# Output projection, second half: where the residual of the meta rows lies and when residual blocks are loaded

## Chip, cores and metric

One NeuronCore of one Trainium2 chip. The time is device microseconds for one execution of the whole program, from the first to the last instruction of the core with what the runtime puts around them. Three runs of the kernel before gave 1338.4, 1341.98 and 1343.84 us.

## What is computed

One decoder layer: a sandwich-normalized mixer of two groups of heads, differential attention and HGRN2, whose outputs are joined and projected, and a convolutional FFN. Sixteen meta rows stand ahead of the 1024 tokens of `x`. The part that matters here is the step from the mixer to the FFN (cut from the reference):

```python
meta = jnp.broadcast_to(meta_tokens[None], (B, N_META, D_MODEL))
h = jnp.concatenate([meta, x], axis=1)                      # 1040 rows of 1024
...
mix = jnp.concatenate([y_diff, y_hgrn], axis=-1) @ w_out[l]
h = h + rmsnorm(mix, ln_mix_post[l])                        # residual of every row
a = rmsnorm(h, ln_ffn_pre[l])
y = conv_ffn(a, w_ffn_up[l], ffn_conv_w[l], ffn_conv_b[l], w_ffn_down[l])
h = h + rmsnorm(y, ln_ffn_post[l])
return h[:, N_META:, :]
```

The FFN's convolution looks two rows back, so of the meta rows only the last two (14 and 15) are needed behind the mixer.

## The kernel before

The rows are worked on in nine blocks: block 0 holds the two meta rows that are still needed, blocks 1 to 8 hold 128 tokens each (`tok`). Every product of f32 values is made of three matmuls, of a high and a low part of each operand (`split`). The mixed rows, split and transposed, lie in DRAM (`msc`); the projection reads them back block by block as `mp` tiles.

The output projection has two halves of 512 columns. The first half (`out_first`) runs beside the last HGRN head. The second half is the loop at line 1218, and is where the change lies. For block i it does, in program order:

- `second_load(i + 1)`: two loads of the next block's `mp` tile. The tiles lie in three places (`SLOTS`), so that block 7 takes the place of block 5 and block 8 that of block 4.
- `run(blocks[i], ...)` over the first four of eight slices of the contraction: 12 matmuls (lines 978, 980, 982).
- `trans(i - 2)`, from i = 4 on: eight transposes on TensorE (line 1171) of the normalized rows `a2` of two blocks before, copied by ACT into the FFN's input `at2`. `trans(1)` comes at i = 3 and `trans(0)` at i = 4.
- `run` over the other four slices.
- `post(i, py)`: the rest of the block's way. ACT takes the sum of squares of the bank `py`, DVE multiplies it by the gain into `tmp`, ACT makes the reciprocal root; DVE adds both halves (`y0` from the first half, `tmp`) to the residual in `xh`, which is then the new `h` and goes to DRAM (`hsc`, line 1151); ACT takes the sum of squares of it; DVE writes the normalized rows `a2`.

At i = 1 the loop also projects block 0, and `out_last(p)` adds the last slice of the first half for each block p (tiles `pz`). `t_split` then splits quarters of `at2` into tiles for the FFN: `t_split(0, 0)` into the place `e0` of the pool `ep`, at i = 5, which has no earlier use.

The residual: `post(i)` makes a tile `xh` (pool `qp`, two buffers) and loads it itself (line 1134). Block 0 has a tile of the same kind, and there `a2` is the tile itself:

```python
        elif i == 0:
            a2 = xh
```

TensorE's instructions stand in the order in which the program writes them (`manual_schedule`). The other engines and SP, from which all these DMAs are issued, get an order of their own from a planner at build time, which goes by program order among what is ready in its own reckoning of time; on the chip each of them then works strictly in that order. A tile that shares a buffer waits until all who used the tile before it are done.

Behind the loop come the first units of the FFN: `plain_unit` (line 1279) and then `unit` (line 1298), whose matmuls of line 1309 wait for DVE to empty their banks (tiles `u`, `uu`, `ug`).

Of the kernel before, what the change touches and what calls it, by code (L numbers as in the profile page):

```python
# [9 lines left out]
F32 = mybir.dt.float32  # L10
# [7 lines left out]
P = 128  # L18
# [3 lines left out]
D = 1024  # L22
# [14 lines left out]
def start(i):  # L37
    return 0 if i == 0 else META + P * (i - 1)
# [47 lines left out]
def layer_kernel(ctx: ExitStack, tc: tile.TileContext, x, meta, table, lbl, gpre, gpost, win,  # L86
# [5 lines left out]
    T, SY = nc.tensor, nc.sync  # L92

    def pool(name, bufs, side="left", space=None):
        kw = {"side": side} if space is None else {"space": space}
        cm = tc.tile_pool(name=name, bufs=bufs, reuse_waits="tile", **kw)
        return cm, cm.__enter__()
# [61 lines left out]
    def rstd_of(dst, ss, n):  # L159
        A.activation(dst, ss, AF.Ln, bias=eps[: dst.shape[0]], scale=1.0 / n)  # L160
        A.activation(dst, dst, AF.Exp, scale=-0.5)
# [3 lines left out]
    def long_tile(name):  # L165
        return mxp.tile([P, 8, WN[0]], F32, tag="X0", name=name).rearrange("p a c -> p (a c)")
# [803 lines left out]
    def tok(i):  # L970
        return (2, 14) if i == 0 else (P, start(i))

    def out_part(m, py, wo, ks, first, last):
        r = m.shape[-1]
        for k in ks:
            hi, lo = wo[k]
            mh, ml = m[:, 0, k], m[:, 1, k]
            T.matmul(py[:r], mh, hi, start=(first and k == ks[0]), stop=False)  # L978
            yield 216
            T.matmul(py[:r], mh, lo, start=False, stop=False)  # L980
            yield 216
            T.matmul(py[:r], ml, hi, start=False, stop=(last and k == ks[-1]))  # L982
            yield 216
# [3 lines left out]
    def block_tile(n, i):  # L987
        tag = SLOTS[n][i - 1]
        if tag == "mp":
            return mlp.tile([P, 2, KD, P], F32R, tag="mp", name=f"mp{n}_{i}")  # L990
        t = mxp.tile([P, 8, WN[0]], F32R, tag=tag, name=f"mp{n}_{i}")
        return t.rearrange("p a c -> p (a c)")[:, : 2 * KD * P].rearrange("p (l k t) -> p l k t", l=2, k=KD)

    def block_load(m, i, k0, k1):
        SY.dma_start(m[:, :, k0:k1].bitcast(F32).rearrange("p l k t -> p l (k t)"), msc[i][:, :, P * k0:P * k1])
# [6 lines left out]
    def second_load(i):  # L1002
        blocks[i] = block_tile(1, i)
        block_load(blocks[i], i, 0, 4)
        block_load(blocks[i], i, 4, 7 if i == 1 else 8)
# [8 lines left out]
    def y0_gain(p):  # L1014
        r = tok(p)[0]
        return G.tensor_tensor(y0[:r, p], y0[:r, p], gpo0[:r], op=ALU.mult)

    def out_last(p):
        r = tok(p)[0]
        py = ps_b(f"pz{p}")  # L1020
        m = m0[:, :, KD - 1:] if p == 0 else k7(p)
        for _ in out_part(m, py, wo0[KD - 1:], range(1), True, True):
            pass
        V.tensor_tensor(y0[:r, p], y0[:r, p], py[:r], op=ALU.add)
        junk = qp.tile([P, 512], F32, tag="junk", name=f"jz{p}", bufs=1)
        A.activation(junk[:r], y0[:r, p], AF.Square, accum_out=ssy[:r, p, 0:1])
        A.activation(ssy[:r, p, 0:1], ssy[:r, p, 0:1], AF.Identity, bias=eps[:r], scale=1.0 / D)
        if p < 3:
            y0_gain(p)
# [24 lines left out]
    def ps_b(name):  # L1054
        return pp.tile([P, 512], F32, tag="b", name=name)
# [3 lines left out]
    e_cm, ep = pool("early", 1, "right")  # L1059
# [7 lines left out]
    q_cm, qp = pool("p2", 2, "right")  # L1067
# [60 lines left out]
    SY.dma_start(gfb, gfpre.to_broadcast([P, D]))  # L1128
    a2t = {}

    def post(i, py):
        r, t0 = tok(i)
        xh = qp.tile([P, D], F32, tag="xh", name=f"xh{i}")
        SY.dma_start(xh[:r], meta[14:16, :] if i == 0 else x[P * (i - 1): P * i, :])
        if i % 2:
            a2 = long_tile(f"a2_{i}")[:, :D]
        elif i == 0:
            a2 = xh
        else:
            a2 = bp.tile([P, D], F32, tag="a2", name=f"a2_{i}", bufs=1)  # L1140
        tmp = qp.tile([P, 512], F32, tag="tmp", name=f"tmp{i}", bufs=1)
        junk = qp.tile([P, 512], F32, tag="junk", name=f"junk{i}", bufs=1)
        s1, s2 = ssy[:r, i, 1:2], ssy[:r, i, 2:3]
        A.activation(junk[:r], py[:r], AF.Square, accum_out=s1)
        V.tensor_tensor(tmp[:r], py[:r], gpo[:r], op=ALU.mult)
        A.activation(s1, s1, AF.Ln, bias=ssy[:r, i, 0:1], scale=1.0 / D)
        A.activation(s1, s1, AF.Exp, scale=-0.5)
        V.scalar_tensor_tensor(xh[:r, :512], y0[:r, i], s1, xh[:r, :512], ALU.mult, ALU.add)
        V.scalar_tensor_tensor(xh[:r, 512:], tmp[:r], s1, xh[:r, 512:], ALU.mult, ALU.add)
        if i:  # L1150
            SY.dma_start(hsc[P * (i - 1): P * i, :], xh)
        if i:
            A.activation(a2[:r], xh[:r], AF.Square, accum_out=s2)
        else:
            s3 = ssy[:r, i, 3:4]
            for half, s_ in ((0, s2), (1, s3)):
                A.activation(py[:r], xh[:r, 512 * half:512 * half + 512], AF.Square, accum_out=s_)
            V.tensor_tensor(s2, s2, s3, op=ALU.add)
        rstd_of(s2, s2, D)
        V.scalar_tensor_tensor(a2[:r], xh[:r], s2, gfb[:r], ALU.mult, ALU.mult)  # L1160
        a2t[i] = a2

    def trans(i):
        r, t0 = tok(i)
        a2 = a2t.pop(i)
        cs = slice(t0 - 14, t0 - 14 + r)
        for half in range(2):
            pt = ps_b(f"pa2_{i}_{half}")
            for j in range(4):
                k = 4 * half + j  # L1170
                T.transpose(pt[:, j * r:(j + 1) * r], a2[:r, P * k: P * (k + 1)], ident[:r, :r])
            pv = pt[:, : 4 * r].rearrange("p (k t) -> p k t", k=4)
            ks = slice(4 * half, 4 * half + 4)
            for p in range(2):
                lo_, hi_ = max(cs.start, C0[p]), min(cs.stop, C0[p] + 2 * WN[p])
                if lo_ < hi_:
                    A.copy(
                        at2[p][:, ks, lo_ - C0[p]:hi_ - C0[p]], pv[:, :, lo_ - cs.start:hi_ - cs.start])
# [10 lines left out]
    def t_split(p, j, src, where, *tag):  # L1189
        hi, lo = t_tiles(p, j, where, tag)  # L1190
        A.copy(hi, src)
        V.tensor_tensor(lo, src, hi.bitcast(F32), op=ALU.subtract)
        tt[p][j] = (hi, lo)

    def quarter(p, j):
        n = WN[p]
        a, c = {0: (0, 0), 7: (0, n), 4: (4, 0), 6: (4, n)}[j]
        return at2[p][:, a:a + 4, c:c + n]
# [12 lines left out]
    def run(*args):  # L1211
        for _ in out_part(*args):
            pass

    def k7(i):
        return m7[:, i - 1:i].rearrange("p b l t -> p l b t")

    for i in range(1, NBLK):
        py = ps_b(f"py1_{i}")
        if i >= 3:  # L1220
            y0_gain(i)
        if i + 1 < NBLK:
            second_load(i + 1)
        run(blocks[i], py, wo, range(4), True, False)
        if i == 3:
            trans(1)
        if i == 4:
            trans(0)
        if i > 3:
            trans(i - 2)  # L1230
        run(blocks[i], py, wo, range(4, 7 if i == 1 else 8), False, i > 1)
        if i == 1:
            pm = ps_b("py1_0")
            run(m0, pm, wo, range(KD), True, True)
            for p in range(3):
                out_last(p)
            run(k7(1), py, wo[KD - 1:], range(1), False, True)
            post(1, py)
            post(0, pm)
            for p in (3, 4):  # L1240
                out_last(p)
            continue
        post(i, py)
        if i == 5:
            t_split(0, 0, quarter(0, 0), ep, "e0")
            t_split(0, 4, quarter(0, 4), ep, "e1")
        if i == 7:
            t_split(0, 7, quarter(0, 7), mxp, "X2", WN[0])
            t_split(0, 6, quarter(0, 6), mxp, "X1", WN[0])
        if i in (2, 3):  # L1250
            for p in (1 + 2 * i, 2 + 2 * i):
                out_last(p)
# [361 lines left out]
```

## Time and profile before

| | us |
|---|---|
| median of three runs | 1341.98 |
| the profiled execution | 1336.17 |
| its span, first to last instruction | 1334.1 |
| TensorE busy | 1287.9 (97%) |
| VectorE busy | 911.1 (68%) |
| ScalarE busy | 692.0 (52%) |
| GpSimd busy | 432.3 (32%) |
| mean granted TensorE clock | 0.995 |

The second half of the projection lies at 587 to 668 us of the span. In the rows of the profile, PE is TensorE, DVE VectorE, ACT ScalarE, POOL GpSimd and SPq the queue of SyncE. A row of the timeline gives the start and the duration in us, the engine, the line, the operation, the tiles as out<-in without their numbers, the shape, and how many instructions are put together; in square brackets stands how long the engine was idle before it and who ended that. `xh` is the residual, `a` the normalized rows `a2`, `py` a bank of the projection, `mp` a block of the mix. Line 53 is a helper through which all instructions of DVE, ACT and POOL go.

### The profile page before, as it was taken

The numbers are of one execution on the slowest core, as the hardware profiler recorded it, in microseconds if no ns is written. First come the engines' busy times: TensorE is split into PE (matmuls) and PEld (weight loads), VectorE is DVE, ScalarE is ACT, GpSimd is POOL, SyncE is SP. The second block draws the span as 40 slices with busy tenths as digits, with TensorE's granted clock in tenths as the row PEclk, the third lists the DMA queues.
The fourth block names the chain that finished last, engine by engine and source line by source line (L and its number), as shares of the span: only waits on it lengthen the run. The fifth ranks groups of instructions, "written<-read, shape, count | busy, mean of one in ns | idle before, by whom it ended". The sixth has DMA issues, their size and how long they took to land.

```text
span 1334.1 us, 26146 instructions
## 1 busy us (share of the span) xinstructions
PE 1287.9 (97%) x10172; PEld 1187.0 (89%) x10172; DVE 911.1 (68%) x1531; ACT 692.0 (52%) x1635; POOL 432.3 (32%) x340
## 2 busy tenths in 40 slices
PE   7999999999999999998998999999999999999997
PEld 6899899989999998677888999999999998878875
DVE  7675657475746574647797687787787776697586
ACT  8465356535654665246665445444445444454453
POOL 5211212121212110334055666666666630010121
PEclk9999999999999999999999999999999999999999
DMA  5331343144311223686412222223222226954253
GB/s 208 123 129 62 116 153 116 56 141 134 111 56 54 82 85 127 194 258 230 144 54 83 95 88 72 74 94 103 87 81 72 82 86 211 326 181 166 88 205 118
DMA packets 99425, 164.99 MB, mean 124 GB/s; under 512 B 10035, under 2 KB 34899, under 8 KB 99302
## 3 DMA queue, kind: packets, MB, share of 16 engines
q1 hardware_dynamic: 99302, 163.32, 35.9%
q8 instruction: 80, 1.31, 0.4%
q14 instruction: 43, 0.35, 0.1%
HBM read 122.65 MB, written 40.63 MB: 122 GB/s over the span
## 4 chain that ended last, share of the span: by engine, by line
PE 46%; DVE 7%; issue 3%; ACT 3%; DMA 2%; POOL 2%; SPq 0%; DVEq 0%; POOLq 0%; ACTq 0%
PE pd L1460 5%; PE pd L1461 5%; PE pd L1459 5%; PE pb L1309 4%; PE pb L1311 4%; PE pb L1310 4%; PE pc L1309 2%; PE pa L1309 2%; PE pa L1311 2%; PE pa L1310 2%; PE pc L1310 2%; PE pc L1311 2%; PE py L982 1%; PE py L980 1%; PE py L978 1%
## 5 line engine op out<-in xcount | busy, mean ns | idle before, releaser
L1309 PE MATMUL pb<-t,uh 128*128 128x258 f32 x504 | 142.9, 284 | 7.7 <-DVE u L53 7.7
L1310 PE MATMUL pb<-t,uh 128*128 128x258 f32 x504 | 141.7, 281 | 0.0
L1311 PE MATMUL pb<-t,ul 128*128 128x258 f32 x504 | 141.5, 281 | 0.0
L1460 PE MATMUL pd<-wl,gh 128*128 128x512 f32 x308 | 122.0, 396 | 0.3 <-DVE wl L53 0.2
L1459 PE MATMUL pd<-wh,gh 128*128 128x512 f32 x308 | 121.6, 395 | 0.0
L1461 PE MATMUL pd<-wh,gl 128*128 128x512 f32 x308 | 121.6, 395 | 0.0
L53 DVE SCALAR_TENSOR_TENSOR c<-uu,cwt,c 128x514 f32<-128x514 f32 (+1 forms) x88 | 97.1, 1104 | 20.6 <-ACT c L53 19.9
L1309 PEld LDWEIGHTS pb<-t,uh 128*128 128x128 f32 x504 | 95.4, 189 | 9.2 <-DVE u L53 8.9
L53 POOL TENSOR_TENSOR c<-c,c 128x514 f32<-128x514 f32 (+1 forms) x44 | 63.4, 1441 | 122.6 <-ACT c L53 118.5
L1310 PEld LDWEIGHTS pb<-t,uh 128*128 128x128 f32 x504 | 95.5, 189 | 0.0
L1311 PEld LDWEIGHTS pb<-t,ul 128*128 128x128 f32 x504 | 95.2, 189 | 0.0
L1309 PE MATMUL pa<-t,uh 128*128 128x258 f32 (+1 forms) x336 | 95.2, 283 | 0.0
L1311 PE MATMUL pa<-t,ul 128*128 128x258 f32 (+1 forms) x336 | 95.0, 283 | 0.0
L1310 PE MATMUL pa<-t,uh 128*128 128x258 f32 (+1 forms) x336 | 94.8, 282 | 0.0
L1309 PE MATMUL pc<-t,uh 128*128 128x258 f32 (+1 forms) x336 | 94.4, 281 | 0.0
L1310 PE MATMUL pc<-t,uh 128*128 128x258 f32 (+1 forms) x336 | 94.0, 280 | 0.0
L1311 PE MATMUL pc<-t,ul 128*128 128x258 f32 (+1 forms) x336 | 93.7, 279 | 0.0
L53 DVE SCALAR_TENSOR_TENSOR c<-ug,cwt,c 128x514 f32<-128x514 f32 (+1 forms) x88 | 86.7, 986 | 2.0 <-ACT c L53 1.4
L53 POOL TENSOR_TENSOR ul<-ws,uh 128x512 fp32r<-128x512 f32 x42 | 61.0, 1453 | 41.1 <-ACT uh L53 36.6
L1460 PEld LDWEIGHTS pd<-wl,gh 128*128 128x128 f32 x308 | 57.7, 187 | 15.5 <-DVE wl L53 1.6
L1459 PEld LDWEIGHTS pd<-wh,gh 128*128 128x128 f32 x308 | 57.7, 187 | 14.1
L1461 PEld LDWEIGHTS pd<-wh,gl 128*128 128x128 f32 x308 | 57.7, 187 | 14.0
(372 smaller groups left out, 4119.4 us busy)
## 6 DMA issues: line engine op xcount, KB each, us to landing
ra<-in_wup_dram SPq DMA_DIRECT2D x88, 256.0 KB, 2.6
mp<-msc SPq DMA_DIRECT2D x23, 512.0 KB, 6.3
wd<-in_wdown_dram SPq DMA_DIRECT2D x44, 256.0 KB, 4.4
tsc<-wd SPq DMA_DIRECT2D x44, 256.0 KB, 2.8
wi<-tsc SPq DMA_DIRECT2D x44, 256.0 KB, 2.8
gi<-gsc SPq DMA_DIRECT2D x33, 256.0 KB, 3.9
wi<-in_wdown_dram SPq DMA_DIRECT2D x33, 256.0 KB, 3.2
gsc<-c SPq DMA_DIRECT2D x22, 257.0 KB, 2.1
```

The source lines that it names most:

```text
L53: ins = call(*args, **kw)
L978: T.matmul(py[:r], mh, hi, start=(first and k == ks[0]), stop=False)
L980: T.matmul(py[:r], mh, lo, start=False, stop=False)
L982: T.matmul(py[:r], ml, hi, start=False, stop=(last and k == ks[-1]))
L1309: T.matmul(pt, hi[:, s], th[:, k], start=(first and k == 0), stop=False, skip_group_check=True)
L1310: T.matmul(pt, hi[:, s], tl[:, k], start=False, stop=False, skip_group_check=True)
L1311: T.matmul(pt, lo[:, s], th[:, k], start=False, stop=(k == 3), skip_group_check=True)
L1459: T.matmul(py, gh[:, s], wh, start=(k == 0 and pr not in (3, 7)), stop=False, skip_group_check=True)
L1460: T.matmul(py, gh[:, s], wl, start=False, stop=False, skip_group_check=True)
L1461: T.matmul(py, gl[:, s], wh, start=False, stop=(k == NH - 1), skip_group_check=True)
```

## The change

The loads of the residual leave `post` for a function of their own, `load_xh`. For block 0 it takes a tile in the place `e0` of the pool `ep` instead of one of the two buffers of `xh`. In the loop it is called one block ahead, behind `second_load(i + 1)`; at i = 1 blocks 1 and 0 are loaded first. `post` takes the tile that it finds. The number of loads, their sizes and the arithmetic stay as they are.

```diff
+    xhs = {}
+
+    def load_xh(i):
+        r = tok(i)[0]
+        if i:
+            xhs[i] = qp.tile([P, D], F32, tag="xh", name=f"xh{i}")
+        else:
+            xhs[i] = ep.tile([P, D], F32, tag="e0", name="xh0")
+        SY.dma_start(xhs[i][:r], meta[14:16, :] if i == 0 else x[P * (i - 1): P * i, :])
+
     def post(i, py):
         r, t0 = tok(i)
-        xh = qp.tile([P, D], F32, tag="xh", name=f"xh{i}")
-        SY.dma_start(xh[:r], meta[14:16, :] if i == 0 else x[P * (i - 1): P * i, :])
+        xh = xhs.pop(i)
...
         py = ps_b(f"py1_{i}")
         if i >= 3:
             y0_gain(i)
+        if i == 1:
+            load_xh(1)
+            load_xh(0)
         if i + 1 < NBLK:
             second_load(i + 1)
+            load_xh(i + 1)
         run(blocks[i], py, wo, range(4), True, False)
```

## The prediction

> **What bounds the kernel now.** I read the page first, for the profiled execution's own time, then the waits of TensorE around the output projection, then TensorE's timeline, the granted clock by stretches, the chain of waits, and the queues of SP, DVE and ACT in the same 80 us.
>
> The page's first line, and TensorE's waits between 580 and 720 us (us in total, times, longest):
>
> ```profile
> span 1334.1 us, 26146 instructions
> ```
>
> ```profile
> PE pb L1309 <- DVE u L53: 6.3, 3, 3.3
> PE pa L1171 <- DVE a L53: 3.8, 2, 3.5
> ```
>
> Two things stop TensorE here: the transposes of line 1171 (`trans`), which wait for the normalized block `a2` from DVE, and, 60 us on, the first FFN units, which wait for DVE to empty a bank. TensorE's timeline shows the first (start, duration, idle before it and who ended it):
>
> ```profile
> 607.26 0.39 PE L978 MATMUL py<-woh,mp 128*128 128x512 f32 x1
> ...
> 613.72 0.40 PE L978 MATMUL pz<-woh,m 128*128 128x512 f32 x1
> ...
> 618.02 0.65 PE L1171 MATMUL pa<-ident,xh 2*128 2x2 f32 x8
> 619.01 1.09 PE L1171 MATMUL pa<-ident,a 128*128 128x128 f32 x8 [0.34 <-DVE a L53]
> ...
> 622.74 0.39 PE L978 MATMUL py<-woh,mp 128*128 128x512 f32 x1
> ...
> 629.18 1.97 PE L1171 MATMUL pa<-ident,a 128*128 128x128 f32 x8 [3.48 <-DVE a L53]
> ...
> 635.51 0.40 PE L978 MATMUL py<-woh,mp 128*128 128x512 f32 x1
> ...
> 638.32 1.03 PE L1171 MATMUL pa<-ident,a 128*128 128x128 f32 x8
> ...
> 641.96 0.40 PE L978 MATMUL py<-woh,mp 128*128 128x512 f32 x1
> ...
> 654.70 0.39 PE L982 MATMUL py<-woh,mp 128*128 128x512 f32 x1
> ```
>
> Blocks 3, 5, 6 and 7 begin at 607.26, 622.74, 635.51 and 641.96; block 3 is over when the `pz` of 613.72 begins. Block 6 takes 641.96 - 635.51 = 6.45 us, block 5 takes 635.51 - 622.74 = 12.77. The 6.32 us between them have two parts. One is the idle time of 3.48 before `trans(3)` at 629.18. The other is in the clock, by stretches (length, busy time of the five engines, granted clock, DMA share, GB/s):
>
> ```profile
> 629.18:634.80 5.62, 5.62 (x18) 4.75 (x19) 2.56 (x3) 2.72 (x6) 0.00 (x0) 0.50 0.59 209
> 634.80:641.90 7.10, 7.10 (x36) 5.89 (x35) 3.00 (x4) 3.58 (x10) 0.00 (x0) 1.00 0.63 211
> ```
>
> After the idle time TensorE runs 5.62 us at a granted clock of 0.50, which loses 5.62 x 0.5 = 2.81. 3.48 + 2.81 = 6.29, the 6.32 but for rounding. [...]
>
> Why `a2` was late, on SP's queue and on DVE:
>
> ```profile
> 589.57 3.13 SPq L995 DMA_DIRECT2D mp<-msc  x4
> 594.03 1.26 SPq L1076 DMA_DIRECT2D ra<-in_wup_dram  x2
> ...
> 608.37 0.33 SPq L1134 DMA_DIRECT2D xh<-in_x_dram  x1
> ...
> 618.98 0.81 SPq L1134 DMA_DIRECT2D xh<-in_x_dram  x2
> ...
> 635.71 1.18 SPq L995 DMA_DIRECT2D mp<-msc  x2
> 638.49 0.33 SPq L1151 DMA_DIRECT2D hsc<-xh  x1
> 638.93 5.51 SPq L1134 DMA_DIRECT2D xh<-in_x_dram  x2
> ```
>
> ```profile
> 606.18 2.16 DVE L53 SCALAR_TENSOR_TENSOR a<-xh,ssy,gfb 128x1024 f32<-128x1024 f32 x1
> ...
> 617.67 1.28 DVE L53 SCALAR_TENSOR_TENSOR a<-xh,ssy,gfb 128x1024 f32<-128x1024 f32 x1 [1.66 <-ACT ssy L53]
> ...
> 623.63 0.75 DVE L53 SCALAR_TENSOR_TENSOR xh<-y,ssy,xh 128x512 f32<-128x512 f32 x1 [3.48 <-DMA xh<-in_x_dram]
> ...
> 640.93 1.28 DVE L53 SCALAR_TENSOR_TENSOR a<-xh,ssy,gfb 128x1024 f32<-128x1024 f32 x1 [2.46 <-ACT ssy L53]
> ...
> 645.37 0.75 DVE L53 SCALAR_TENSOR_TENSOR xh<-y,ssy,xh 128x512 f32<-128x512 f32 x1 [1.80 <-DMA xh<-in_x_dram]
> ```
>
> `xh` has two buffers. The meta rows (`xh0`) hold one until `trans(0)` at 618.02, since for block 0 `a2` is `xh` itself. So blocks 1, 2 and 3 pass through the other: `xh2` goes out at 608.37, as `a2` of block 1 ends (606.18 + 2.16 = 608.34); `xh3` at 618.98, as `a2` of block 2 ends (617.67 + 1.28 = 618.95). DVE then waits 3.48 for `xh3`, and TensorE 3.48 for what comes of it. The chain of waits holds this load and a later one:
>
> ```profile
> 618.98 4.43 DMA xh<-in_x_dram
> ...
> 638.93 6.32 DMA xh<-in_x_dram
> ```
>
> **The change, part by part.** The number of DMAs and of instructions on every engine stays as it is: nine residual loads, eight of 512 KB. What moves is where they stand and which buffer they take.
>
> *Meta tile.* `xh0` goes to `e0`, idle until `t_split(0, 0)`. That split now waits for `trans(0)`; its cast runs at 622.09 (below), 4 us behind 618.02, so this is 0. `xh1` and `xh0` go ahead of block 2's weights of the mix instead of behind them, which puts one 512 KB load in front of these.
>
> ```profile
> 580.00:590.00 10.00, 10.00 (x45) 8.06 (x44) 0.92 (x2) 4.00 (x7) 4.60 (x4) 1.00 0.91 265
> ```
>
> ```profile
> DMA to landing us min/median/max: 4.2/6.3/9.0
> ```
>
> The DMA engines are nearly full there: 512 KB at 265 GB/s take 2.0 us, and the `mp` loads land in 6.3 at the median and 9.0 at most. `xh2` now finds a free buffer and also goes out near 589, ahead of block 3's and 4's `mp` (589.57) and of two `ra` loads (594.03). The last of the four `mp` is issued by 589.57 + 3.13 = 592.7 and lands by 592.7 + 9.0 + 2.0 = 603.7, before block 3 starts at 607.26: 0. The `ra` loads feed GpSimd's weight sums, which stand before two gains on `y`:
>
> ```profile
> 607.22 3.52 POOL L53 TENSOR_TENSOR y<-y,gpo 128x512 f32<-128x512 f32 x2
> ```
>
> At 2.0 later these end at 607.22 + 3.52 + 2.0 = 612.7, and block 3 is over only at 613.72: 0. If that cover were gone, block 3's `a2` would be late by as much, and has 5 us to spare (next).
>
> *Block 3.* `xh3` takes the buffer of `xh1`, free at 608.34, and lands by 608.37 + 4.43 = 612.8, ahead of its projection at 613.72. Block 5 shows the chain from there with no stall of TensorE: over at 635.51, its `a2` done at 640.93 + 1.28 = 642.21, 6.70 later. So `a2` of block 3 is done at about 613.72 + 6.70 = 620.4, and `trans(3)`, at 625.7 (629.18 - 3.48), no longer waits. Gone are 3.48 and the 2.81 of clock. The 0.34 before `trans(2)` at 619.01 goes too, for `xh2` is there 20 us earlier. Sum on TensorE: 6.63.
>
> *What is late next.* `trans(4)`, at 638.32, comes at 631.7. Should `a2` of block 2 still end at 618.95, `xh4` goes out then, lands at 623.4 to 625.3 (4.43 and 6.32), and by block 5's steps behind a landed residual (about 5.2 us: two adds, square, rstd, scale) `a2` of block 4 is done at 628.6 to 630.5. That leaves 1.2 us or more. From block 4 on each load waits for `a2` of two blocks before, now as before; only its place on SP is earlier.
>
> *DVE behind it.* The second load of the chain, at 638.93, stood behind the store of 638.49 on SP, though the `a2` that frees its buffer was older; DVE waits 1.80 for it at 645.37. Asked for one block ahead it should stand in front of that store, and the 1.80 go. What this is worth shows on ACT:
>
> ```profile
> 622.09 2.02 ACT L53 CAST t<-at 128x1032 fp32r<-128x1032 f32 x2
> ...
> 646.82 1.06 ACT L53 ACTIVATE a<-xh 128x1024 f32<-128x1024 f32 x1 [3.41 <-DVE xh L53]
> ...
> 655.75 0.58 ACT L53 ACTIVATE junk<-py 128x512 f32<-128x512 f32 x1
> ```
>
> ACT's square of block 6 (646.82) moves by 1.80, but block 8's first step (655.75) can't come before the last matmul of block 8 ends (654.70 + 0.39 = 655.09). So this chain, which feeds the `t` splits on DVE and through them the 6.3 us of waits in the FFN units, gains 0.66 at that point. Bounds: 0, if the planned order of DVE keeps the wait, to 1.80, if splits that need no block 8 use all of it. I take 0.66, since that row is the last gate.
>
> Sum: 6.63 + 0.66 = 7.3 us. The profiled execution took 1336.17 (its span of 1334.1 and 2.07 around it), so it would take 1328.9. The median of the runs shown is 1341.98, 5.8 above that execution; nothing here touches this difference, so the forecast is 1341.98 - 7.3 = 1334.7. A measurement of this kernel can tell about 0.5% from no change, 6.7 us: the sum lies just beyond it.
>
> **The rivals.**
>
> *Only the buffer counts.* SP's order comes from a planner and goes by when a buffer comes free; then residuals 4 to 8 don't move, the 1.80 stays, and the gain is 6.63: 1335.3. For: the loads at 608.37 and 618.98 left within 0.03 us of the release. Against: the one at 638.93 did not.
>
> *A mix load starves.* Block 7's `mp` goes out at 635.71 because its buffer is block 5's, and is needed at 641.96; 6.25 us are no more than the median landing of 6.3. If `xh6` now stands in front of it, its 512 KB cost up to 2.0 us: a gain of 5.3, 1336.7. [...]
>
> [...]
>
> *Slower.* The early load stands on SP waiting for an `a2`, and the `mp` loads of the next block stand behind it. From the point where this holds an `mp` for the 3.48 of idle time that dropped the clock, each such block costs what block 5 did, 6.3. At blocks 6 and 7 both that is 12.6 against 6.6 saved: +6, 1348; with a third block +12. Against it: the `a2` that such a load waits for is due 1.2 us before its transposes.
>
> **How the numbers follow.** Forecast 0.45; only the buffer 0.17; a mix load starves 0.15; half cured or given back 0.13; slower 0.10. The forecast's own range is 1332.5 (1.80 for 0.66, and 1 us of scatter) to 1337. The range to name reaches down 2 us further for what the DVE chain may still yield, 1330, and up to no gain, 1343. The forecast and "only the buffer" lie on both sides of 0.5% with the scatter of the runs (1338.4 to 1343.84): three quarters of the one and half of the other count as faster, 0.34 + 0.08 = 0.42; the slower case counts whole, 0.10; what is left of the first two and the two cases between, 0.48, is within 0.5%. Above 1343 lies little but the slower case; with a gain over 12 us and scatter the range leaves out less than 2 in 10.
>
> **What would show it.** Right: no idle time before `trans(3)`, a granted clock of 1.00 throughout the projection, block 5 in about 6.5 us, the third residual load on SP near 589 and the fourth near 608.4, `trans(0)` no longer before a residual load, and the first FFN matmul some 6.6 us earlier. The sum is wrong if TensorE waits at another block, above all for `mp` of block 7, if DVE still waits for a residual near 639, or if the waits for `u` in the FFN units grow by what the projection saved.

## The result, and the profile after

| | before | after |
|---|---|---|
| median, us (22 runs each) | 1340.45 | 1337.41 |
| lowest and highest | 1336.26 to 1347.05 | 1332.36 to 1342.53 |
| the profiled execution | 1336.17 | 1337.66 |
| its span | 1334.1 | 1335.8 |
| mean granted clock in it | 0.995 | 0.992 |

The ratio is 0.9975, with a 95% interval of 0.9963 to 0.9986: the changed kernel is faster by 0.25%, about 3 us, between 1.9 and 5.0. The forecast was a gain of 7.3 us, and a change of no more than 0.5% was called the likeliest. Two profiled executions can't show this: here the trace of after is the longer one by 1.7 us. So the stage has to be read by itself.

The page's first line, and TensorE's waits between 580 and 725 us (us in total, times, longest):

```profile
span 1335.8 us, 26154 instructions
```

```profile
PE pb L1322 <- DVE u L53: 6.1, 3, 3.6
PE pa L1180 <- DVE a L53: 0.8, 1, 0.8
```

The wait of the transposes has fallen from 3.8 to 0.8 us; that of the FFN units for `u` is where it was. TensorE's timeline, with the lines that answer to those of before (`trans` is line 1180 now; the first FFN matmul is the `pq`):

```profile
622.95 0.40 PE L978 MATMUL py<-woh,mp 128*128 128x512 f32 x1
...
625.85 0.65 PE L1180 MATMUL pa<-ident,xh 2*128 2x2 f32 x8
626.43 1.09 PE L1180 MATMUL pa<-ident,a 128*128 128x128 f32 x8
...
630.15 0.40 PE L978 MATMUL py<-woh,mp 128*128 128x512 f32 x1
...
632.96 1.09 PE L1180 MATMUL pa<-ident,a 128*128 128x128 f32 x8
...
636.68 0.39 PE L978 MATMUL py<-woh,mp 128*128 128x512 f32 x1
...
640.48 1.09 PE L1180 MATMUL pa<-ident,a 128*128 128x128 f32 x8 [0.84 <-DVE a L53]
...
644.21 0.39 PE L978 MATMUL py<-woh,mp 128*128 128x512 f32 x1
...
657.18 0.28 PE L1303 MATMUL pq<-t,uh 128*128 128x258 f32 x1
```

`trans(2)` at 626.43 and `trans(3)` at 632.96 show no idle time before them. Block 5 takes 636.68 - 630.15 = 6.53 us, where it took 12.77. Block 6 takes 644.21 - 636.68 = 7.53, where it took 6.45: a new wait of 0.84 stands before `trans(4)`. The clock, by stretches (the same columns as before, of the trace after; the first two lines are far ahead of the change, the last two run from `trans(2)` to `trans(4)`):

```profile
29.00:34.00 5.00, 5.00 (x19) 4.81 (x20) 2.13 (x7) 2.64 (x9) 0.00 (x0) 0.50 0.01 2
177.00:184.00 7.00, 5.05 (x19) 4.96 (x20) 4.32 (x8) 1.34 (x3) 0.00 (x0) 0.56 0.29 111
626.00:633.00 7.00, 7.00 (x41) 5.71 (x40) 4.78 (x4) 4.60 (x14) 2.95 (x2) 1.00 0.72 259
633.00:640.40 7.40, 6.63 (x33) 5.22 (x32) 5.57 (x7) 5.75 (x16) 0.00 (x0) 1.00 0.82 275
```

The half clock behind `trans(3)` is gone. But this execution ran at half clock near 29 and 179 us, where the program, instruction for instruction on TensorE, is that of before. The trace of before ran there at full clock:

```profile
29.00:34.00 5.00, 4.99 (x33) 4.93 (x34) 3.69 (x10) 4.36 (x16) 0.00 (x0) 1.00 0.01 2
174.00:180.00 6.00, 4.64 (x33) 4.61 (x34) 3.83 (x8) 1.86 (x5) 0.00 (x0) 1.00 0.37 142
```

That is most of why block 4 starts at 622.95 here and at 615.12 there: the two traces differ by up to 0.7 us ahead of the first of these places, by 2.3 us behind it and by 6.1 behind the second. A time "us from the start" can't be compared between these two traces without taking off 7.83; lengths within the stage can.

The residual loads on SP's queue, and DVE's steps on them (start, duration, idle before):

```profile
595.11 0.54 SPq L1139 DMA_DIRECT2D xh<-in_x_dram  x1
596.99 0.59 SPq L1139 DMA_DIRECT2D xh<-in_x_dram  x1
...
615.50 0.33 SPq L1139 DMA_DIRECT2D xh<-in_x_dram  x1
...
624.57 0.33 SPq L1139 DMA_DIRECT2D xh<-in_x_dram  x1
...
637.81 1.26 SPq L995 DMA_DIRECT2D mp<-msc  x2
...
640.74 0.34 SPq L1139 DMA_DIRECT2D xh<-in_x_dram  x1
```

```profile
614.21 1.27 DVE L53 SCALAR_TENSOR_TENSOR a<-xh,ssy,gfb 128x1024 f32<-128x1024 f32 x1
...
622.58 1.96 DVE L53 SCALAR_TENSOR_TENSOR a<-xh,ssy,gfb 128x1024 f32<-128x1024 f32 x1 [1.10 <-ACT ssy L53]
...
625.66 0.68 DVE L53 TENSOR_TENSOR tmp<-py,gpo 128x512 f32<-128x512 f32 x1
626.26 1.53 DVE L53 SCALAR_TENSOR_TENSOR xh<-y,ssy,xh 128x512 f32<-128x512 f32 x1
627.72 1.78 DVE L53 SCALAR_TENSOR_TENSOR xh<-tmp,ssy,xh 128x512 f32<-128x512 f32 x1
631.62 1.29 DVE L53 SCALAR_TENSOR_TENSOR a<-xh,ssy,gfb 128x1024 f32<-128x1024 f32 x1 [2.12 <-ACT ssy L53]
633.05 2.38 DVE L53 TENSOR_TENSOR t<-at,t 128x1032 fp32r<-128x1032 f32 x2
635.35 0.68 DVE L53 TENSOR_TENSOR tmp<-py,gpo 128x512 f32<-128x512 f32 x1
635.95 0.74 DVE L53 SCALAR_TENSOR_TENSOR xh<-y,ssy,xh 128x512 f32<-128x512 f32 x1
...
639.13 1.29 DVE L53 SCALAR_TENSOR_TENSOR a<-xh,ssy,gfb 128x1024 f32<-128x1024 f32 x1 [1.78 <-ACT ssy L53]
```

`xh1` and `xh2` go out within 2 us of each other, `xh3` at 615.50, as `a2` of block 1 ends (614.21 + 1.27 = 615.48). No row of DVE in the stage waits for a residual any more. The row at 631.62 is `a2` of block 3: it ends at 632.91, and `trans(3)` begins at 632.96, so it came with nothing to spare. The last line is `a2` of block 4: it ends at 640.42, and `trans(4)` begins at 640.48.

### The profile page after: what moved, and what is told of

Its sections match the earlier page's. It is cut to its first block, busy times and chain, and to the rows that moved or that the text cites. A ratio compares the mean times of both kernels' runs of the same rounds, so it can differ in the third digit from the quotient of the medians.

```text
span 1335.8 us, 26154 instructions
## 1 busy us (share of the span) xinstructions
PE 1291.0 (97%) x10172; PEld 1190.5 (89%) x10172; DVE 909.3 (68%) x1531; ACT 693.4 (52%) x1635; POOL 435.7 (33%) x340
## 4 chain that ended last, share of the span: by engine, by line
PE 67%; DVE 8%; ACT 4%; DMA 3%; issue 3%; POOL 2%; SPq 1%; DVEq 0%; ACTq 0%; POOLq 0%
PE pd L1473 5%; PE pd L1472 5%; PE pd L1474 5%; PE pb L1322 4%; PE pb L1324 4%; PE pb L1323 4%; PE pa L1322 3%; PE pa L1324 3%; PE pa L1323 3%; PE pc L1322 2%; PE pc L1323 2%; PE pc L1324 2%; PE pa L710 2%; DMA wd<-in_wdown_dram 2%; PE py L982 1%
```

## The experiments

Two questions were open. What gains: the buffer that the meta rows held (the meta tile alone), or also the load one block ahead and its place on SP? And where did half of the 7.3 us go: into a half clock that was counted too dear because it comes by lot, into the new wait at `trans(4)`, or back into the waits for `u` in the FFN units? Where an expectation calls a theory by a letter, its figures there say which of these it is. In the stage table, times are us from the first matmul of block 4 to the first FFN matmul, all on TensorE; "half clock" is how long the stage ran at 0.50.

| kernel | stage | block 5 | block 6 | half clock |
|---|---|---|---|---|
| before (the prediction's trace) | 39.81 | 12.77 | 6.45 | 6.8 |
| before, second trace | 37.64 | 11.02 | 6.45 | 3.4 |
| before, third trace | 38.88 | 11.77 | 6.45 | 3.4 |
| before, operands later | 39.99 | 11.51 | 6.44 | 3.4 |
| only the load ahead | 37.37 | 10.77 | 6.45 | 3.4 |
| eight idle matmuls at `trans(3)` | 37.78 | 10.05 | 6.47 | 0 |
| only the meta tile | 34.36 | 6.56 | 7.51 | 0 |
| after | 34.23 | 6.53 | 7.53 | 0 |
| after, second trace | 34.42 | 6.73 | 7.51 | 0 |
| after, splits one block later | 34.52 | 6.84 | 7.51 | 0 |
| after, twelve matmuls more in the FFN | 34.89 | 7.21 | 7.52 | 0 |
| after, operands later | 34.57 | 6.88 | 7.51 | 0 |
| after, casts behind the square | 35.08 | 6.84 | 8.07 | 0 |
| after, both later edits | 35.12 | 6.88 | 8.09 | 0 |

### The kernel before, once more

> The kernel before, unchanged, for a second trace and for the granted clock of each run. Theory A (the half clock of 2.81 us behind the wait for trans(3) is there in every execution): the trace shows an idle time of about 3.5 us ahead of trans(3), 5 to 7 us at a granted clock of 0.50 behind it, and block 5 takes about 12.8 us. [...]

1340.79 us, ratio 0.9992 (0.9976 to 1.0009): the same program against itself, so an interval of this width is what 12 runs can tell. Its trace, at the same place:

```profile
624.28 1.09 PE L1171 MATMUL pa<-ident,a 128*128 128x128 f32 x8
...
633.70 1.85 PE L1171 MATMUL pa<-ident,a 128*128 128x128 f32 x8 [2.74 <-DVE a L53]
```

```profile
633.70:637.40 3.70, 3.70 (x13) 3.27 (x14) 1.27 (x2) 2.37 (x5) 0.00 (x0) 0.54 0.72 200
```

The wait is 2.74 instead of 3.48, and the half clock lasts half as long, 3.41 instead of 6.83 us. So the row from which the prediction took 2.81 us was one case of several, and a dear one.

### Eight idle matmuls before `trans(3)`, in the kernel before

```diff
+            if i == 3 and half == 0:
+                for _ in range(8):
+                    T.matmul(pt, blocks[5][:, 0, 0], wo[0][0], start=True, stop=True)
```

The bank that they fill is overwritten by the transposes.

> The kernel before with eight matmuls of 128x512 (about 1.9 us), whose result is overwritten, ahead of trans(3), in the time in which TensorE waits there. The wait for a2 stays, the idle time falls from 3.5 to about 1.6 us. Theory A (half clock in every execution): 2.8 us faster than before, ratio 0.9979, and granted clock 1.00 behind trans(3). Theory B (half clock only in some): 0 to 1.5 us faster, ratio 0.9989 to 1.000. If the eight matmuls delay the transposes themselves: slower by up to 1.9 us.

1338.09 us, 0.998 (0.9964 to 0.9996).

```profile
633.12 2.03 PE L1171 MATMUL pa<-woh,mp 128*128 128x512 f32 x8
636.63 1.09 PE L1174 MATMUL pa<-ident,a 128*128 128x128 f32 x8 [1.49 <-DVE a L53]
```

The transposes still come when `a2` is there, but no half clock follows in this trace, and block 5 is the shortest of the kernels with the late load. The half clock is thus a price of its own, and in this one trace it went without any change to the loads; the measured time can't confirm it, since its interval holds both theories.

### Only the meta tile

```diff
-        xh = qp.tile([P, D], F32, tag="xh", name=f"xh{i}")
+        xh = qp.tile([P, D], F32, tag="xh", name=f"xh{i}") if i else ep.tile([P, D], F32, tag="e0", name="xh0")
```

> Only the first half of the change: the meta rows' residual in e0, the loads where they were, inside post. Theory 'only the buffer counts': the planner sends a load as soon as its buffer is free, so xh2 goes out with xh1 near 590, xh3 as a2 of block 1 ends, no wait ahead of trans(3); time as with the whole change, ratio 0.9975 within 0.001. Theory 'place in the program counts too': the later residuals, above all block 6's, stand behind a store and DVE waits 1 to 2 us for one near 645; up to 1 us slower than the whole change.

1339.12 us, 0.9983 (0.9964 to 1.0001).

```profile
633.12 1.10 PE L1171 MATMUL pa<-ident,a 128*128 128x128 f32 x8
...
640.63 1.09 PE L1171 MATMUL pa<-ident,a 128*128 128x128 f32 x8 [0.82 <-DVE a L53]
```

```profile
DVE xh L53 <- DMA xh<-in_x_dram: 1.5, 1, 1.5
```

On TensorE the stage is that of after, the new wait included, 34.36 to 34.23. DVE still waits 1.5 us for one residual, and nothing on TensorE shows it in the stage. The interval of the time can't separate it from after or from before; the trace does.

### Only the load ahead

```diff
+        xhs[i] = qp.tile([P, D], F32, tag="xh", name=f"xh{i}")
...
+        if i == 1:
+            load_xh(1)
+            load_xh(0)
...
+            load_xh(i + 1)
```

> Only the second half of the change: residuals loaded one block ahead, the meta rows still in one of the two buffers of xh. Theory 'only the buffer counts': xh2 still waits for a2 of block 1 and xh3 for a2 of block 2, idle time of about 3.5 us ahead of trans(3), ratio 1.000 within 0.001. Theory 'place in the program counts': part of the gain, ratio 0.998 to 0.999, from loads that no longer stand behind stores and mix loads on SP.

1339.72 us, 0.9987 (0.9969 to 1.0004).

```profile
632.49 1.97 PE L1177 MATMUL pa<-ident,a 128*128 128x128 f32 x8 [2.69 <-DVE a L53]
```

```profile
DVE xh L53 <- DMA xh<-in_x_dram: 4.1, 2, 2.9
```

The wait of TensorE, the half clock and DVE's two waits for residuals are all still there, as in the second trace of before. The ratio lies between the two expectations and its interval holds both, so the trace has to tell them apart. In the stage, asking earlier changes nothing while both buffers are held: the buffer is what gains.

### The changed kernel, once more

> The whole change, unchanged, for a second trace. Theory 'typical stall': the wait for trans(3), which the profile of before showed at its longest (3.48 idle, 6.83 us of half clock), costs 10.8 to 11.0 us of block 5 at other times, and the change replaces it by a wait of 0.8 us at trans(4); blocks 4 to 8 take 34.2 us against 37.4 to 37.8, and the time is 3.0 to 3.5 us below before, ratio 0.9975 within 0.0012. Theory 'the gain is there and given back later': blocks 4 to 8 take 6 us less than in the kernel before and the FFN units grow by 3.

1337.08 us, 0.9973 (0.9956 to 0.999).

```profile
637.23 1.09 PE L1180 MATMUL pa<-ident,a 128*128 128x128 f32 x8 [0.83 <-DVE a L53]
```

The second trace repeats the stage to 0.2 us, the wait of 0.83 too. But `trans(3)` is not free of waits: in the five traces of the changed kernel with a later edit it waits 0.16 to 0.52 us, with block 5 at 6.84 to 7.21. The longest, of the kernel with twelve matmuls more:

```profile
632.73 1.09 PE L1180 MATMUL pa<-ident,a 128*128 128x128 f32 x8 [0.52 <-DVE a L53]
```

### The quarter splits one block later

```diff
-        if i == 5:
+        if i == 6:
             t_split(0, 0, quarter(0, 0), ep, "e0")
```

> The whole change, and the split of the FFN quarters (0, 0) and (0, 4) emitted behind block 6 instead of block 5. Theory 'the new wait at trans(4) comes of the order on ACT and DVE': the two casts of 2.0 us no longer stand ahead of block 4's sum of squares, trans(4) waits 0, blocks 4 to 8 take 33.2 us, 0.8 to 1.0 us faster than the whole change. Theory 'it comes of the residual load of block 4': the wait of 0.8 us stays.

1337.96 us, 0.9981 (0.9966 to 0.9995), and the wait at `trans(4)` is 0.83. The edit told nothing: in the kernel as built, ACT's casts stand where they stood, since the planner goes by what is ready and not by the line alone.

### The casts behind the square of block 4

```diff
-        A.activation(junk[:r], py[:r], AF.Square, accum_out=s1)
+        squares_of[i] = A.activation(junk[:r], py[:r], AF.Square, accum_out=s1)
...
+            with tc.issue_after(squares_of[4].ins):
+                t_split(0, 0, quarter(0, 0), ep, "e0")
+                t_split(0, 4, quarter(0, 4), ep, "e1")
```

This one does move them. In the changed kernel ACT's order is casts first, then the square of block 4:

```profile
631.96 2.02 ACT L53 CAST t<-at 128x1032 fp32r<-128x1032 f32 x2
633.86 0.60 ACT L53 ACTIVATE junk<-py 128x512 f32<-128x512 f32 x1
```

> The whole change, with the two casts of the FFN quarters (0, 0) and (0, 4) put behind block 4's sum of squares in ACT's order. Moving their place in the program by one block had left ACT's order as it was, so it told nothing. Theory 'the wait at trans(4) comes of ACT's order': the wait of 0.83 us falls below 0.3, blocks 4 to 8 take 33.4 to 33.7 us against 34.2 to 34.4, and the time falls by 0 to 0.8 us. Theory 'it comes of the residual load of block 4': the wait stays at 0.8 us.

1338.38 us, 0.9977 (0.996 to 0.9993), and the wait went up.

```profile
640.95 1.09 PE L1180 MATMUL pa<-ident,a 128*128 128x128 f32 x8 [1.42 <-DVE a L53]
```

```profile
635.81 0.75 DVE L53 SCALAR_TENSOR_TENSOR xh<-y,ssy,xh 128x512 f32<-128x512 f32 x1
...
639.01 0.69 DVE L53 TENSOR_TENSOR tmp<-py,gpo 128x512 f32<-128x512 f32 x1 [1.79 <-ACT junk L53]
639.62 1.28 DVE L53 SCALAR_TENSOR_TENSOR a<-xh,ssy,gfb 128x1024 f32<-128x1024 f32 x1
```

With the casts gone from in front, the planner set the next block's `tmp` ahead of block 4's `a2`, and DVE stood 1.79 us for that block's square. So `a2` came later by another road. This supports that the order on ACT and DVE decides when `a2` of block 4 is done; it does not show that the casts are the cause of the 0.84 in the changed kernel. The residual is not its cause: it left at 624.57 in the changed kernel, and the slowest landing in the prediction's rows (6.32) would have it there at 630.9, five us before the add at 635.95.

### Twelve matmuls more in an FFN unit

```diff
+        if (ft, p) == (2, 1):
+            mm(2, pc, True)
         mm(2, pc, True)
```

One call of `mm` is twelve matmuls; what the first call writes is overwritten by the second.

> The whole change, with twelve matmuls more (1.4 us) at the second FFN tile, whose result is overwritten, in the time in which TensorE waits 3.3 to 3.6 us for u near 715. Theory 'half clock by lot': the idle time falls to about 2.0 us, the half clock of 3.4 to 6.8 us that four of six traces show there goes, 1.5 to 2.5 us faster than the whole change. Theory 'the half clock there costs nothing, since DVE is what is late': same time within 1 us.

1337.26 us, 0.9978 (0.9963 to 0.9994). The wait for `u` near 715 us is 2.11, where the other traces without the operands' edit have 3.2 to 3.6, but 3.4 us of half clock still follow it and the time is that of the changed kernel. A shorter wait was not enough there.

### The down projection's first operands later

The long wait for `u` near 715 us is common to both kernels. The waits of the changed kernel between 580 and 725 us name where it begins:

```profile
ACT gh L53 <- DMA gi<-gsc: 9.3, 2, 5.5
DVE gl L53 <- ACT gh L53: 7.2, 2, 3.7
```

`gi` is an operand of the down projection, loaded and split far ahead, in the middle of the FFN units; ACT and DVE stand for it while TensorE's banks wait to be emptied. The edit orders the first of these loads behind the store of a late FFN unit:

```diff
-            with tc.high_priority() if i == 0 else nullcontext():
+            with tc.issue_after(stores[NF - 3, 1].ins) if i < LOOK else nullcontext():
                 ready[i] = operands(*steps[i])
```

> The whole change, with the first operands of the down projection (four loads from gsc and their splits) issued behind the store of FFN tile 19 instead of right behind that of their own tile, so that ACT and DVE no longer wait 3.2 to 3.7 us for each in their fixed order near 702, 720 and 743. Theory 'the FFN waits come of these loads': the wait for u near 715 goes from 3.5 to below 1.5 us with its half clock, 3 to 5 us faster than the whole change. Theory 'DVE is full there anyway': under 1 us faster, the wait for u stays over 2.5 us.

1332.84 us (6 runs), 0.994 (0.9923 to 0.9957): the fastest version, 4.2 us under the changed kernel on the same chip. TensorE's waits between 580 and 800 us:

```profile
PE pb L1322 <- DVE u L53: 2.5, 2, 1.4
```

About the first ten FFN units (the first 864 matmuls of `unit`) take 105.77 us instead of 112.23 in the changed kernel, 6.5 less. The rest of the program takes 544.54 instead of 541.67, 2.9 more: the operands' loads now begin at 1072 us, and between 1077 and 1094 TensorE has three new waits for `u`, 1.8 us in total.

### Both later edits, and the operands' edit on the kernel before

> The whole change with both edits that touch a wait: the first operands of the down projection behind the store of FFN tile 19, and the two casts behind block 4's sum of squares. If the two add up: ratio 0.9935 within 0.0015, about 0.5 to 0.8 us below the first edit alone (0.994). If DVE takes back what ACT's order gives: the same as the first edit alone.

1334.42 us, 0.997 (0.9949 to 0.9991): both expectations were missed, since each named about 0.994. Against the casts' edit alone, on the same chip, the median is 4.0 us lower, but the two ratios, 0.997 and 0.9977, are only about 1 us apart. The wait near 715 us is gone here too. The casts' edit adds nothing; how much the operands' edit is worth beside it stays open.

> The kernel before, without the change, with the first operands of the down projection behind the store of FFN tile 19. If the gain of that edit and of the change add up: 4.0 to 4.5 us below before, ratio 0.9968 within 0.0015, and blocks 4 to 8 take 37.4 us or more with the wait for trans(3). If the change's gain came back partly in the FFN waits: the edit gives 5 us or more here and less on top of the change.

1339.46 us, 0.9993 (0.9971 to 1.0015): a miss. Its one trace is of its dearest execution, 1345.82 us, with 17 us of half clock ahead of block 4; it has the same first FFN units at 106.21 us, as hoped, but the rest at 545.36 and the stage at 39.99. Why the median lacks the gain as well can't be read from it. Whether the two gains add up stays open: on top of the whole change the operands' edit gave 4.2 us (6 runs), without the change none that can be measured.

### The kernel before, a third trace

> The kernel before once more, for a third trace of its stall. Theory 'typical stall': idle time ahead of trans(3) 2.7 to 3.0 us, one half-clock stretch of 3.4 us or none, blocks 4 to 8 in 36.5 to 37.8 us. Theory 'every execution as the one predicted from': idle 3.5 us, 6.8 us of half clock, 39.8 us.

One execution, 1344.07 us.

```profile
636.08 1.31 PE L1171 MATMUL pa<-ident,a 128*128 128x128 f32 x8 [3.53 <-DVE a L53]
```

An idle time of 3.53, longer than the prediction's 3.48, and behind it 3.41 us of half clock, not 6.83. The length of the half clock does not follow from that of the wait.

## Why the prediction was right or wrong

**The mechanism: right.** The buffer that the meta rows held was the cause. On the trace that the prediction read, the stage lost 39.81 - 34.23 = 5.58 us, and the new wait lengthens block 6 by 7.53 - 6.45 = 1.08: together 6.66, where the sum had 6.63 for idle time and clock. So the sum was right for that one execution, which has the dearest of the three stages of before.

**"Gone are 3.48 and the 2.81 of clock": right as a place, mis-sized as a term.** Three traces of before have 3.48, 2.74 and 3.53 of idle time. The half clock behind it covers 5.66, 3.41 and 3.41 us of TensorE's work, and what block 5 takes beyond its wait and the 6.45 of block 6 is 2.84, 1.83 and 1.79 us, about half of that. Block 5 takes 12.77, 11.02 and 11.77, a mean of 11.85. In the five traces of the changed kernel in which the order on ACT and DVE is the same, it takes 6.53, 6.73, 6.84, 7.21 and 6.88, a mean of 6.84: 5.0 is what goes there as a rule. The 0.34 before `trans(2)` is likewise in some traces only: block 4 takes 7.62, 7.20 and 7.72, against 7.20 or 7.21; mean gain 0.3.

**"Block 3": five us to spare were reckoned, and there were none.** The prediction had `a2` of block 3 done at 620.4, which is 628.2 in the trace of after, 6.70 us behind its projection, as in block 5. It was done at 632.91, 11.4 us behind it. The residual was there in time, but the square of block 3 began on ACT 2.2 us behind the projection (623.73), its `tmp` stood on DVE until 625.66, behind `a2` of block 2 and an add to `y`, and its two adds took 3.2 us, where those of block 5 in the trace of before took 1.4; GpSimd was busy on `y` for most of the 3.2, and whether that is the reason was not tested. That `trans(3)` still found `a2` ready, by 0.05 us, was luck.

**"What is late next": this step failed.** It gave `a2` of block 4 at least 1.2 us to spare, from the landing of `xh4` and block 5's steps behind a landed residual. `xh4` in fact went out 2.2 us earlier than this (624.57, where 618.95 + 7.83 = 626.8 was reckoned), and `trans(4)` would have come at 639.64, where 631.7 + 7.83 = 639.5 was reckoned. But block 4's `a2` did not follow its residual: its square on ACT stood behind two casts until 633.86, its `tmp` on DVE behind `a2` of block 3 and two splits until 635.35. For both blocks the steps had been copied from block 5 of the trace of before, for whose projection ACT stood idle for 2.33 us and DVE for 1.73; blocks that follow each other without a stall meet the fixed order of ACT and DVE instead. The wait is 0.84, 0.83, 0.82 and 0.82 in after, its second trace, the kernel with only the meta tile, and that with the later operands. It costs 1.1, by block 6. This comes nearest to what the list of chances calls "half cured", and the stage of these four traces has no half clock. How short a wait has to be for the full clock was not shown: half clock came behind 1.6 us of idle time near 28 us in the trace of after and behind 2.74 in the second trace of before, and none behind 3.30 in the first.

**The sum over the stage.** 5.0 + 0.3 - 1.1 = 4.2 us; the stage table gives the same, a mean of 38.78 before and 34.53 in those five traces. The measured gain, 1.9 to 5.0, holds it. What lies between 4.2 and the 3.0 of the medians is less than the scatter of one execution. The time itself came out 2.7 us above the forecast of 1334.7, although the gain fell short by 4.3: the forecast started from the median of three runs, 1341.98, and that of 22 is 1.5 lower. That part of the nearness is luck.

**DVE behind it, 0.66: about right in size, and not the change's alone.** The first wait for `u` is 1.60, 1.34 and 1.69 in the traces of before and 1.08 and 1.06 after, 0.5 less; the second is 1.42 or 1.43 in all five. With only the load ahead, where DVE still waited for residuals, the two are 1.06 and 1.42; with only the meta tile there is one wait of 2.05 in place of both, with 3.41 us of half clock behind it. So each half alone shortens these waits by as much, and the small gain is not tied to the 1.80 that went. The long wait for `u` did not grow: 3.30, 3.54 and 3.30 before, 3.56 and 3.28 after.

**The rivals.** *Only the buffer counts*: true on TensorE in the stage, by the two half kernels; it was named as the lesser case and described the gain best, though with the whole change DVE's wait of 1.80 for the residual of block 6 did go, as the forecast's own case had it. Its reckoned gain of 6.63 has the same mis-sized term. *A mix load starves*: no; block 7's `mp` goes out at 637.81, ahead of the `xh` at 640.74, and block 7 takes 6.48 in both kernels. *Slower*: no. The second halves of the `mp` loads of blocks 5, 6 and 8 do go out right behind a residual that had waited (615.88, 624.95 and 633.33), but no row of TensorE waits for `mp`. *Given back in the FFN*: no; the first 864 matmuls of `unit` take 112.37, 113.57 and 113.72 in the traces of before and 112.23 and 111.88 after.

## What to carry to other kernels

When a prefetch comes late, find who holds its buffer before moving the request: freeing the buffer gave all of the stage's gain here, asking earlier none of it. Whether a wait brings a half clock, and how long a one, differs from one execution to the next (at `trans(3)` 3.48, 2.74 and 3.53 us brought 6.83, 3.41 and 3.41; the 3.30 before `u` in the first of these traces brought none), so take its price from several traces of the same program, and compare stages and not spans. When a stall goes, work out the next blocks from the fixed order of every engine on their way, not from the steps of a block that stood behind a stall.

## What was not expected of the hardware

The same program at the same place runs at half clock in one execution and at full clock in another, for 3.41 or 6.83 us at a time. In the trace of after this happened near 28 us behind 1.6 us of idle time and near 179 behind 3.1, in that of before at neither (1.65 and 1.47 us of idle time there). The first matmul of block 4 starts between 615.12 and 627.39 us over all fourteen traces, though the same 5344 matmuls stand ahead of it in all, and the time of one kernel spreads over some 10 us. An idle time of 3.53 us brought 3.41 us of half clock and one of 3.48 brought 6.83, so the cost can't be read from the wait alone. TensorE's waits and the half clock behind them, in us:

| trace, wait | idle before | half clock |
|---|---|---|
| before, `trans(3)` | 3.48 | 6.83 |
| before, second trace, `trans(3)` | 2.74 | 3.41 |
| before, third trace, `trans(3)` | 3.53 | 3.41 |
| before, `u` near 715 | 3.30 | 0 |
| after, `u` near 717 | 3.56 | 3.41 |

The 3.30 us before `u` cost no clock, while the 2.74 at `trans(3)` did. What decides between the two was not tested.
